# Turning the gated outputs with VectorE's 32x32 transposes instead of TensorE's, with a layout made by DMA

## The chip, the cores and the metric

The kernel runs on one core of a Trainium2 chip. The metric is the device time of one execution in microseconds (us), as the median of several runs; lower is better. The engines of a core work side by side, each in the order of its own queue: TensorE (PE for matmuls, PEld for its weight loads), VectorE (DVE), ScalarE (ACT), GpSimd (POOL) and SyncE (SP), which here issues nearly all DMAs.

## The reference

One layer of a streaming encoder over a prompt of 4096 frames and a sample of 64 frames, width 1024, in float32. What matters here is the end of the layer:

```
o_a = rms_norm(o_a, g_on_gla).reshape(B, T, 512) * silu(z_a)      # GLA branch, 4 heads of 128
o_h = rms_norm(o_h, g_on_hgrn).reshape(B, T, 512) * silu(z_h)     # HGRN2 branch, 4 heads of 128
o   = einsum('bte,ed->btd', concatenate([o_a, o_h]), w_out)       # w_out is 1024 x 1024
y   = x + gate * rms_norm(o, g_post)
```

`g_on_gla` and `g_on_hgrn` are gains of 128 values, the same for each head of their branch. Before that stand the adaLN modulation, one input projection and two chunked recurrences.

## The kernel before, in words

Matrix products run in fp32r on numbers split in two parts: `hi` is the rounded value (a cast on ACT), `lo` the rest (a subtraction, on DVE or POOL), and a product takes three matmuls (hi x w_hi, hi x w_lo, lo x w_hi). The function `split` (L84) makes both parts.

Frames are worked on in tiles of 128, two to a group of 256: 32 tiles of the prompt and one of 64 frames for the sample, which rides with the third group. There are three phases.

- Phase 1 (up to about 900 us) projects and runs the GLA recurrence. Its outputs, normalised without their gain and already multiplied by silu(z_a), are stored to DRAM as `oa_d` (L1109).
- Phase 2 (up to about 1600 us) does the same for HGRN2. Its outputs, normalised without gain and without silu(z_h), go to `oh_d`. While its last group is finished, the generator `load_wout` (L1198) loads w_out in 16 halves of [128 x 512] through the staging tiles `wst`, and splits each (the cast on ACT, L90; the rest on POOL, L91). In the same stretch the z projection of the first four tiles runs (`until(4)`).
- Phase 3 (`phase3`, L1218) goes tile by tile. `z_tile` (L1185) computes silu(z_h) of a tile some five tiles ahead: 24 matmuls (L571), a sigmoid on ACT (L1193) and a product on DVE (L1194) into a tile `e`. `load` brings the tile's GLA and HGRN outputs into `og` (L1215, L1216) and x into `xt`. `turn` (L1241) multiplies the HGRN half by `e` (L1244, called og*e below), turns the tile from frames on partitions to features on partitions with eight 128x128 TensorE transposes into two PSUM banks (`ps_tp`, `ps_ms`, L1252), and splits the result into `ogh` and `ogl`, with the gain of the output norm as a scalar per partition (L87, L88). Then come 48 matmuls with w_out (L1287) into two `pj` banks, a sum of squares on ACT (L1292), the products with the gate (L1296), rsqrt by Newton steps (L71 to L81), the sum with x (L1299) and the store of y (L1303).

The phases overlap by generators that are advanced in turn (`weave`). A scheduler in the framework orders the instructions of each engine: it takes the program's order as priority, and what is ready by its own estimate of durations. That order is fixed when the kernel is built; on the chip each queue goes strictly in it and waits where an operand is late. Tiles come from pools with a fixed number of buffers, and an instruction that writes a new tile waits until the tile that had this buffer is read for the last time. Numbers that matter: `og`, `ogh`, `ogl`, `y`, `xt` two buffers each, `e` five, PSUM `pj` three banks, `at` two (the z projection in phase 3). The buffers of phase 3 use the memory of the recurrences' tiles, so they are free only when phase 2 has ended.

Of the kernel before, what the change touches and what calls it, by code (L numbers as in the profile page):

```python
# [6 lines left out]
F32 = mybir.dt.float32  # L7
# [4 lines left out]
ALU = mybir.AluOpType  # L12
# [3 lines left out]
P = 128  # L16
# [12 lines left out]
class Kernel:  # L29
# [1167 lines left out]

    def load_wout(self, out):  # L1198

        sts = []  # L1200
        for i in range(2 * KT + 2):
            if i < 2 * KT:
                kt, n = divmod(i, 2)
                st = self.wst()[:, :512]
                self.nc.sync.dma_start(st, self.t["w_out"][0, kt * P : (kt + 1) * P, 512 * n : 512 * n + 512])
                sts.append(st)
            if i >= 2:
                out.append(self.split_w(sts[i - 2], "wv" if i - 2 < 8 else "wu", self.nc.gpsimd))
            yield

    def og_load(self, tile, og):

        g, j, (kind, _, r, _) = tile
        g = g if kind == "p" else -1
        self.nc.sync.dma_start(og[:r, :512], self.oa_d[g][j])  # L1215
        self.nc.sync.dma_start(og[:r, 512:], self.oh_d[g][j])  # L1216

    def phase3(self, tiles, zgen, og):  # L1218
        nc, t = self.nc, self.t
        with ExitStack() as s:  # L1220
            one = self.pool(s, "p3one")
            ap = self.pool(s, "p3a")
            gg = one.tile([P, 2, D], F32, name="gg")
            for i in range(2):
                nc.sync.dma_start(gg[:, i, :], self.gate_d[i : i + 1, :].to_broadcast([P, D]))
            Wo = self.W3["o"]
            og0 = og

            def load(i):
                g, j, (kind, r0, r, o) = tiles[i]  # L1230
                if i > 0:
                    og = ap.tile([P, D], F32, name="og", bufs=2)
                    self.og_load(tiles[i], og)
                else:
                    og = og0
                xt = self.xp.tile([P, D], F32, name="xt", bufs=2)
                src = t["x_prompt"] if kind == "p" else t["x_sample"]
                nc.sync.dma_start(xt[:r], src[0, r0 : r0 + r, :])
                return og, xt

            def turn(i, og):  # L1241
                r = tiles[i][2][2]
                e = self.zq.pop(0)
                nc.vector.tensor_tensor(og[:r, 512:], og[:r, 512:], e, ALU.mult)  # L1244
                hi = ap.tile([P, D], F32R, name="ogh", bufs=2).rearrange("p (k c) -> p k c", k=KT)
                lo = None
                if r == P:
                    lo = ap.tile([P, D], F32R, name="ogl", bufs=2).rearrange("p (k c) -> p k c", k=KT)
                for q, tag in enumerate(("tp", "ms")):
                    pt = self.ps(tag).rearrange("p (k c) -> p k c", k=4)  # L1250
                    for k in range(4):
                        nc.tensor.transpose(  # L1252
                            pt[:, k, :r], og[:r, (4 * q + k) * P : (4 * q + k + 1) * P], self.ident[:r, :r]
                        )
                    ks = slice(4 * q, 4 * q + 4)
                    self.split(hi[:, ks, :r], lo[:, ks, :r] if r == P else hi[:, ks, r : 2 * r], pt[:, :, :r], gain=self.col[:, 50 + q : 51 + q])
                return hi, lo

            n = len(tiles)
            og, xt = load(0)  # L1260
            next(zgen, None)
            hl = turn(0, og)
            for i in range(n):
                g, j, (kind, r0, r, o) = tiles[i]
                dst = t["y_prompt"] if kind == "p" else t["y_sample"]
                x_now, (hi, lo) = xt, hl
                if i + 1 < n:
                    next(zgen, None)
                    og, xt = load(i + 1)
                    hl = turn(i + 1, og)  # L1270
                cnd = 0 if kind == "p" else 1
                ss = self.small.tile([P, 2], F32, name="y_ss")[:r]
                y = ap.tile([P, D], F32, name="y", bufs=2)
                if i == n - 1:

                    self.tc.keep_in_program_order(nc.scalar.preload_act_table_set("natural_log_exp_and_others"))
                for q in range(2):
                    po = self.ps("pj")
                    cs = slice(512 * q, 512 * q + 512)
                    m = 0  # L1280
                    for kt in range(KT):
                        wh, wl = Wo[2 * kt + q][:, 0], Wo[2 * kt + q][:, 1]
                        if r < P:
                            self.pair_step(po, hi[:, kt, : 2 * r], r, wh, wl, kt)
                            continue
                        for a, b in ((hi, wh), (hi, wl), (lo, wh)):
                            nc.tensor.matmul(po[:r], a[:, kt, :r], b, start=m == 0, stop=m == 3 * KT - 1)  # L1287
                            m += 1
                    if r < P:
                        self.fold(po, r, 512, y[:, cs])  # L1290
                    junk = ap.tile([P, 512], mybir.dt.bfloat16, name="sq", bufs=1)[:r]
                    nc.scalar.activation(junk, po[:r], AF.Square, accum_out=ss[:, q : q + 1])  # L1292
                    if q:
                        nc.vector.tensor_tensor(ss[:, 0:1], ss[:, 0:1], ss[:, 1:2], ALU.add)
                        rs = self.rstd(ss[:, 0:1], D, table=i == n - 1)
                    nc.vector.tensor_tensor(y[:r, cs], po[:r], gg[:r, cnd, cs], ALU.mult)  # L1296
                for q in range(2):
                    cs = slice(512 * q, 512 * q + 512)
                    nc.vector.scalar_tensor_tensor(y[:r, cs], y[:r, cs], rs, x_now[:r, cs], ALU.mult, ALU.add)  # L1299
                    if i == n - 1:  # L1300
                        (nc.scalar if q else nc.sync).dma_start(dst[0, r0 : r0 + r, cs], y[:r, cs])
                if i < n - 1:
                    nc.sync.dma_start(dst[0, r0 : r0 + r, :], y[:r])  # L1303
# [189 lines left out]
```

## Time and profile before

| | |
|---|---|
| median of 3 runs | 2168.68 us (2168.2 to 2170.03) |
| the profiled execution | 2167.58 us, its span 2165.8 us |
| granted clock of TensorE | 0.995 of full speed on the mean |
| PE busy | 2121.3 us, 98% of the span |
| DVE / ACT / POOL busy | 1448.8 / 979.4 / 237.1 us |
| PE transposes in phase 3 (L1252), recorded | 256, of 264 issued |
| DMA engines, mean share busy | 24% by the main queue |

The page of the profile has parts: busy time by engine, the span in slices, the DMA queues, the chain of work that ended last (followed back from the last instruction to whatever released each step), the costliest groups of instructions, and DMA issues. A row of a group reads: line, engine, operation, output<-inputs, shapes, count, busy us and mean ns of one, then the idle time before them and what ended it. A row of a timeline reads: start in us from the span's start, duration, engine, line, operation, operands, count, and in brackets how long the engine had been idle and for what. A row of the chain reads: start, length, engine or DMA, tile, line, count.

### The profile page before, as it was taken

What the parts mean: (1) busy time and instruction counts of PE and PEld (TensorE: products, weight loads), DVE (VectorE), ACT (ScalarE), POOL (GpSimd) and SP (SyncE); (2) the same over time, 40 slices, a digit from 0 to 9 for tenths busy, and PEclk for the clock granted to TensorE, in tenths of its full rate; (3) what the DMA queues carried; (4) which work ended last, traced back from release to release, by engine and by line L of the source; (5) the groups of instructions that cost most, each with busy time, mean ns of one, the idle gap of its engine ahead of it and who ended that gap; (6) DMA issues with size and microseconds to landing.
All of it is one profiled execution on the core that took longest, in us unless ns stands there. A gap on an engine that the chain in (4) does not pass through costs nothing.

```text
span 2165.8 us, 44469 instructions
## 1 busy us (share of the span) xinstructions
PE 2121.3 (98%) x16776; PEld 1868.9 (86%) x16776; DVE 1448.8 (67%) x4735; ACT 979.4 (45%) x2790; POOL 237.1 (11%) x636
## 2 busy tenths in 40 slices
PE   7999999999999999999999999999989999999998
PEld 6898899999999888889899988999868888888887
DVE  6866666666666687777778877677894454545444
ACT  5665555655556564434444444444542222222212
POOL 3200010000110111110111111000230000000000
PEclk9999999999999999999999999999999999999999
DMA  9321111211111231011121111001343433333322
GB/s 269 118 76 55 55 50 60 79 55 55 50 60 65 89 102 42 30 40 58 58 70 46 35 31 50 31 31 42 99 151 119 127 128 107 127 112 131 109 102 87
DMA packets 98706, 173.15 MB, mean 80 GB/s; under 512 B 12668, under 2 KB 34656, under 8 KB 98492
## 3 DMA queue, kind: packets, MB, share of 16 engines
q1 hardware_dynamic: 98348, 170.05, 24.1%
q8 instruction: 132, 2.16, 0.4%
q14 instruction: 82, 0.67, 0.1%
q10 hardware_dynamic: 144, 0.26, 0.0%
HBM read 118.35 MB, written 51.93 MB: 79 GB/s over the span
## 4 chain that ended last, share of the span: by engine, by line
PE 86%; DVE 7%; ACT 3%; DMA 3%; issue 1%; POOL 0%; SPq 0%; DVEq 0%; ACTq 0%; POOLq 0%
PE ps_pj L571 22%; PE ps_pj L559 22%; PE ps_pj L1287 16%; PE ps_at L571 7%; PE ps_at L908 2%; PE ps_ms L791 2%; PE ps_at L638 2%; PE ps_o L775 2%; PE ps_o L770 2%; DMA xt<-in_x_prompt_dram 2%; DVE wst L861 1%; PE ps_tp L506 1%; PE ps_at L718 1%; PE ps_tp L745 1%; PE ps_pj L579 1%
## 5 line engine op out<-in xcount | busy, mean ns | idle before, releaser
L571 PE MATMUL ps_pj<-wu,hh 128*128 128x512 f32 x1632 | 405.3, 397 | 3.3 <-DVE hh L91 2.4
L559 PE MATMUL ps_pj<-hh,wu 128*128 128x256 f32 (+1 forms) x2976 | 395.6, 287 | 0.0
L559 PEld LDWEIGHTS ps_pj<-hh,wu 128*128 128x128 f32 x2976 | 373.8, 191 | 4.6 <-issue 0.3
L571 PEld LDWEIGHTS ps_pj<-wu,hh 128*128 128x128 f32 x1632 | 297.6, 188 | 65.5 <-issue 3.5
L559 PE MATMUL ps_pj<-hh,wv 128*128 128x256 f32 (+1 forms) x1536 | 214.1, 289 | 0.0
L559 PEld LDWEIGHTS ps_pj<-hh,wv 128*128 128x128 f32 x1536 | 192.5, 188 | 14.9 <-issue 12.9
L571 PE MATMUL ps_pj<-wv,hh 128*128 128x264 f32 x1464 | 203.2, 290 | 1.6 <-DVE wv L91 1.6
L571 PEld LDWEIGHTS ps_pj<-wv,hh 128*128 128x128 f32 x1464 | 184.5, 188 | 6.5 <-issue 3.1
L1292 ACT ACTIVATE sq<-ps_pj 128x512 bf16<-128x512 f32 (+1 forms) x66 | 39.4, 597 | 294.7 <-PE ps_pj L1287 289.7
L1287 PE MATMUL ps_pj<-wv,ogh 128*128 128x512 f32 x512 | 163.0, 399 | 0.0
L571 PE MATMUL ps_at<-wu,hh 128*128 128x512 f32 x672 | 158.5, 392 | 0.0
L1287 PE MATMUL ps_pj<-wu,ogh 128*128 128x512 f32 x512 | 157.9, 390 | 0.0
L90 ACT CAST hh<-hf 128x512 fp32r<-128x512 f32 (+1 forms) x188 | 117.7, 626 | 75.2 <-PE ps_pj L571 36.8
L571 PEld LDWEIGHTS ps_at<-wu,hh 128*128 128x128 f32 x672 | 126.9, 189 | 26.4
L91 DVE TENSOR_TENSOR hh<-hf,hh 128x512 fp32r<-128x512 f32 (+1 forms) x188 | 133.1, 710 | 14.2 <-ACT hh L90 12.8
L1153 ACT ACTIVATE g<-ps_pj 128x256 f32<-128x256 f32 (+1 forms) x128 | 49.4, 386 | 198.2 <-PE ps_pj L559 197.7
L861 DVE TENSOR_TENSOR wst<-wst,T 128x160 f32<-128x160 f32 (+4 forms) x480 | 118.1, 263 | 4.0
L1287 PEld LDWEIGHTS ps_pj<-wu,ogh 128*128 128x128 f32 x512 | 96.1, 188 | 20.7
L890 POOL COPY T<-T 128x16 f32<-128x16 f32 (+1 forms) x32 | 9.6, 299 | 942.3 <-DVE Qg L831 870.4
L1287 PEld LDWEIGHTS ps_pj<-wv,ogh 128*128 128x128 f32 x512 | 94.4, 189 | 19.1
L1287 PE MATMUL ps_pj<-wv,ogl 128*128 128x512 f32 x256 | 100.7, 394 | 0.0
L1287 PE MATMUL ps_pj<-wu,ogl 128*128 128x512 f32 x256 | 99.7, 390 | 0.0
(300 smaller groups left out, 3705.7 us busy)
## 6 DMA issues: line engine op xcount, KB each, us to landing
xt<-in_x_prompt_dram SPq DMA_DIRECT2D x64, 512.0 KB
hf<-h_d SPq DMA_DIRECT2D x128, 256.0 KB
h_d<-hf SPq DMA_DIRECT2D x64, 256.0 KB
out_y_prompt_dram<-y SPq DMA_DIRECT2D x31, 512.0 KB
wst<-in_w_in_dram SPq DMA_DIRECT2D x36, 256.0 KB
ada_st<-in_w_ada_dram SPq DMA_DIRECT2D x32, 256.0 KB
oa_d<-e SPq DMA_DIRECT2D x32, 256.0 KB
oh_d<-e SPq DMA_DIRECT2D x32, 256.0 KB
```

The costliest lines, as they stand in the source:

```text
L90: self.nc.scalar.copy(hi, src)
L91: (eng or self.nc.vector).tensor_tensor(lo, src, hi.bitcast(F32), ALU.subtract)
L559: self.nc.tensor.matmul(ps[:, :T], a, b, start=i == 0, stop=i == n - 1)
L571: self.nc.tensor.matmul(ps[:r, : c1 - c0], a, b, start=kt == 0 and i == 0, stop=kt == KT - 1 and i == 2)
L638: nc.tensor.transpose(pt[:, i * P : (i + 1) * P], D[:, c + i, :], self.ident)
L770: nc.tensor.matmul(po[h], A[:, c * 4 + h, :], v, start=h < n, stop=St is None and h == 4 - n)
L775: nc.tensor.matmul(o, Q[rows[s], c * G + g, :], St[rows[s], g, :], start=NS == 2 and not apart and h == 1, stop=h == 4 - NS or h == 3 and ...
L791: nc.tensor.matmul(pd[s * w : (s + 1) * w, g, :], kc[:CL, g, s * w : (s + 1) * w], vs[c][:CL, h * P : (h + 1) * P], start=not apart, stop= ...
L861: nc.vector.tensor_tensor(parts(dst), parts(src), t.unsqueeze(3).to_broadcast(shape), ALU.mult)
L908: nc.tensor.matmul(pas[s][rows, g0 + g], K[rr, 2 * pr + g, rows], Yt[rr, o : o + P], start=True, stop=True)
L1153: nc.scalar.activation(sg, pf[:, :T], AF.Sigmoid)
L1287: nc.tensor.matmul(po[:r], a[:, kt, :r], b, start=m == 0, stop=m == 3 * KT - 1)
```

## The change

The eight TensorE transposes of a tile are replaced. A 128x128 turn is done as a layout step between the quarters of 32 partitions, and a turn inside each 32x32 block. For the GLA half the layout step is made as the tile is loaded: four DMAs instead of one, each for 32 partitions, with pieces of 512 bytes, bring `og[32a+t, 128b+f] = oa[32b+t, 128a+f]`. The HGRN half must first be multiplied by `e` in the layout of frames, so its layout step comes after that product: 16 DMAs from SBUF to SBUF (32 partitions x 512 bytes each) into a new tile `oq` with one buffer. Then one VectorE transpose of 32x32 blocks for each half writes `oT` [128 x 512] (one buffer for both halves), and `split` reads that from SBUF instead of PSUM.

The features come out in another order: partition 32a+i of feature tile c holds feature 128a+32c+i of its half. w_out's rows are loaded in the same order, by four DMAs of 32 rows for each half-tile instead of one of 128. Since partitions of a feature tile no longer share the heads' gain index in the same way, the gain is no longer a scalar in `split`; it is loaded in the new order into a small tile (eight DMAs into 8 columns of an `e` tile) and multiplied into the w_out half on GpSimd, in place, before its split.

```diff
     def load_wout(self, out):
+        nc, t = self.nc, self.t
+        gain = self.etile()[:, :8]
+        for q, name in enumerate(("g_onorm_gla", "g_onorm_hgrn")):
+            src = t[name].rearrange("o (c i) -> i (o c)", c=4)
+            for a in range(4):
+                nc.sync.dma_start(gain[32 * a : 32 * a + 32, 4 * q : 4 * q + 4], src)
+        src = t["w_out"][0].rearrange("(q a c i) n -> q c a i n", q=2, a=4, c=4)
...
-                self.nc.sync.dma_start(st, self.t["w_out"][0, kt * P : (kt + 1) * P, 512 * n : 512 * n + 512])
+                for a in range(4):
+                    nc.sync.dma_start(st[32 * a : 32 * a + 32], src[kt // 4, kt % 4, a][:, 512 * n : 512 * n + 512])
                 sts.append(st)
             if i >= 2:
-                out.append(self.split_w(sts[i - 2], "wv" if i - 2 < 8 else "wu", self.nc.gpsimd))
+                st = sts[i - 2]
+                kt = (i - 2) // 2
+                nc.gpsimd.tensor_scalar(st, st, gain[:, kt : kt + 1], None, ALU.mult)
+                out.append(self.split_w(st, "wv" if i - 2 < 8 else "wu", nc.gpsimd))
...
     def og_load(self, tile, og):
-        self.nc.sync.dma_start(og[:r, :512], self.oa_d[g][j])
+        src = self.oa_d[g][j].rearrange("(b t) (a f) -> a t b f", t=32, a=4)
+        for a in range(4):
+            self.nc.sync.dma_start(
+                og[32 * a : 32 * a + 32, : r // 32 * P].rearrange("p (b f) -> p b f", f=P), src[a]
+            )
         self.nc.sync.dma_start(og[:r, 512:], self.oh_d[g][j])
...
             def turn(i, og):
                 r = tiles[i][2][2]
+                nb = r // 32
                 e = self.zq.pop(0)
                 nc.vector.tensor_tensor(og[:r, 512:], og[:r, 512:], e, ALU.mult)
+                oq = ap.tile([P, 512], F32, name="oq", bufs=1)
+                for a in range(4):
+                    for b in range(nb):
+                        nc.sync.dma_start(
+                            oq[32 * a : 32 * a + 32, b * P : b * P + P],
+                            og[32 * b : 32 * b + 32, 512 + a * P : 512 + a * P + P],
+                        )
...
-                for q, tag in enumerate(("tp", "ms")):
-                    pt = self.ps(tag).rearrange("p (k c) -> p k c", k=4)
-                    for k in range(4):
-                        nc.tensor.transpose(
-                            pt[:, k, :r], og[:r, (4 * q + k) * P : (4 * q + k + 1) * P], self.ident[:r, :r]
-                        )
+                for q, src in enumerate((og, oq)):
                     ks = slice(4 * q, 4 * q + 4)
-                    self.split(hi[:, ks, :r], ..., pt[:, :, :r], gain=self.col[:, 50 + q : 51 + q])
+                    oT = ap.tile([P, 512], F32, name="oT", bufs=1)[:, : 4 * r].rearrange("p (k c) -> p k c", k=4)
+                    nc.vector.transpose(
+                        oT.rearrange("p c (b t) -> p b c t", t=32),
+                        src[:, : nb * P].rearrange("p (b c i) -> p b c i", b=nb, i=32),
+                    )
+                    self.split(hi[:, ks, :r], ..., oT)
                 return hi, lo
```

More of the change, by code (lines that the diff above doesn't have):

```diff
@@ L1248, in turn @@
                     lo = ap.tile([P, D], F32R, name="ogl", bufs=2).rearrange("p (k c) -> p k c", k=KT)
-                for q, tag in enumerate(("tp", "ms")):
-                    pt = self.ps(tag).rearrange("p (k c) -> p k c", k=4)
-                    for k in range(4):
-                        nc.tensor.transpose(
-                            pt[:, k, :r], og[:r, (4 * q + k) * P : (4 * q + k + 1) * P], self.ident[:r, :r]
-                        )
-                    ks = slice(4 * q, 4 * q + 4)
-                    self.split(hi[:, ks, :r], lo[:, ks, :r] if r == P else hi[:, ks, r : 2 * r], pt[:, :, :r], gain=self.col[:, 50 + q : 51 + q])
+                for q, src in enumerate((og, oq)):
+                    ks = slice(4 * q, 4 * q + 4)
+                    oT = ap.tile([P, 512], F32, name="oT", bufs=1)[:, : 4 * r].rearrange("p (k c) -> p k c", k=4)
[3 more added lines that the diff above has]
+                    )
+                    self.split(hi[:, ks, :r], lo[:, ks, :r] if r == P else hi[:, ks, r : 2 * r], oT)
                 return hi, lo
```

## The prediction

> **What bounds the kernel now.** I read the page first (busy shares, then the chain that ended last), then a table of busy time by stretch to see where TensorE (PE) has room.
>
> ```profile
> PE 2121.3 (98%) x16776; PEld 1868.9 (86%) x16776; DVE 1448.8 (67%) x4735; ACT 979.4 (45%) x2790; POOL 237.1 (11%) x636
> PE 86%; DVE 7%; ACT 3%; DMA 3%; issue 1%; POOL 0%; SPq 0%; DVEq 0%; ACTq 0%; POOLq 0%
> ...
> 1540.00:1605.00 65.00, 58.77 (x423) 47.82 (x421) 61.35 (x148) 37.17 (x97) 25.69 (x31) 0.97 0.40 125
> 1605.00:1626.00 21.00, 17.31 (x76) 14.70 (x77) 15.90 (x45) 8.52 (x21) 5.78 (x11) 0.83 0.58 180
> ...
> 1700.00:1900.00 200.00, 200.00 (x929) 164.61 (x927) 101.04 (x278) 52.48 (x110) 0.00 (x0) 1.00 0.36 119
> ...
> 2088.00:2136.00 48.00, 48.00 (x231) 39.91 (x230) 21.80 (x64) 10.53 (x24) 0.00 (x0) 1.00 0.36 121
> ```
>
> The columns of the stretches are: length, busy time of PE, PEld, DVE, ACT, POOL, granted clock, DMA share, GB/s. The change lies in the last part (phase 3, from about 1615 us) and in the stage before it, where w_out is loaded. In phase 3 PE has no idle time at the full clock (200.00 of 200.00), DVE is half busy, POOL is empty. In 1540 to 1626 it is otherwise: DVE is 61.35 of 65 busy there and PE waits. So PE time taken away counts fully in phase 3, and nowhere else is there a promise. The chain shows what one tile costs:
>
> ```profile
> 1909.54 5.44 PE ps_at L571 x24
> 1914.98 0.44 PE ps_tp L1252 x4
> 1915.42 0.44 PE ps_ms L1252 x4
> 1915.86 10.98 PE ps_pj L1287 x48
> 1926.84 5.44 PE ps_at L571 x24
> ...
> 2112.58 10.98 PE ps_pj L1287 x48
> 2123.56 0.44 PE ps_tp L1252 x4
> 2124.00 0.44 PE ps_ms L1252 x4
> 2124.44 10.99 PE ps_pj L1287 x48
> ```
>
> A tile is 24 matmuls of the z projection, 8 transposes, 48 matmuls with w_out: 17.30 us from z to z. The last tiles have no z: 11.86 us. The transposes take 0.88 us of each.
>
> **The change, part by part.**
>
> *The eight TensorE transposes go.* 33 tiles; those of tiles 0 and 1 lie in the entry to phase 3, which I cost apart. 31 x 0.88 = 27.3 us off the path, if PE finds its operands in time. The period would be 16.42 us, and 10.98 in the tail. What must stay inside that:
>
> ```profile
> 1862.87 0.34 SPq L1303 DMA_DIRECT2D out_y_prompt_dram<-y  x1
> ...
> 1863.99 0.53 SPq L1215 DMA_DIRECT2D og<-oa_d  x1
> 1864.56 1.21 SPq L1216 DMA_DIRECT2D og<-oh_d  x1
> ...
> 1870.12 0.69 DVE L1244 TENSOR_TENSOR og<-og,e 128x512 f32<-128x512 f32 x1 [4.36 <-DMA og<-oh_d]
> 1870.73 0.68 DVE L1296 TENSOR_TENSOR y<-ps_pj,gg 128x512 f32<-128x512 f32 x1
> ...
> 67.44 1.25 SPq L404 DMA_DIRECT2D e<-in_w_alpha_dram  x3
> ...
> 2101.12 0.42 SPq L1216 DMA_DIRECT2D og<-oh_d  x1
> 2104.39 0.69 DVE L1244 TENSOR_TENSOR og<-og,e 128x512 f32<-128x512 f32 x1
> ...
> L91 DVE TENSOR_TENSOR hh<-hf,hh 128x512 fp32r<-128x512 f32 x24 | 16.4, 685 | 0.3 <-issue 0.3
> L88 DVE SCALAR_TENSOR_TENSOR ogl<-ps_ms,col,ogh 128x512 fp32r<-128x512 f32 x11 | 8.1, 740 | 0.0
> L90 ACT CAST hh<-hf 128x512 fp32r<-128x512 f32 x24 | 15.0, 624 | 11.4 <-PE ps_at L571 11.4
> ...
> q1 hardware_dynamic: 98348, 170.05, 24.1%
> ```
>
> *SP's queue.* Small DMAs follow each other every 1.25 / 3 = 0.42 us. A tile now issues 6 (y store, x load, two og loads, two of h on the mean); it will issue 25 (og in 5, and 16 for `oq`): 10.5 us of 16.42. In the tail 23, 9.7 us of 10.98: full, but it fits. Without its cover it would cost what it lies over.
>
> *DVE.* 101.04 / 200 x 17.30 = 8.74 us a tile. Two transposes of 128x512 are in no row; the nearest is the 685 ns of a two-input operation SBUF to SBUF of that shape (L91). Below I allow half of it, above twice; I take 0.69 each, since shape and memory are the same: +1.4 us. The low parts go from 740 ns to L91's 685: -0.1. So 10.0 us of 16.42, hidden under PE, and 11.4 with both at twice that. ACT's casts read SBUF in place of PSUM, at the 624 ns that L90 takes from there: nothing to pay. The Trainium skill ("VectorE: DVE Perf Modes", section "The three transpose paths") gives 311 ns for a 128x128 bf16 transpose on VectorE; four of these make an estimated 1.24 us, and DVE would need 11.1 us: the sum is the same. No run so far shows it.
>
> *The DMA engines.* 24.1% of 16 engines over 2165.8 us for 98348 packets is 85 ns a packet. 384 more packets for og (512 B instead of 2 KB) and 512 for oq are at most 896 x 85 / 16 = 4.8 us a tile, above the 36% now: about two thirds. No bound.
>
> *The new wait.* The transpose of the HGRN half waits for 16 DMAs: 16 x 0.42 = 6.7 us of issue, plus landing, which the rows at 2101.12 and 2104.39 put at no more than 2.85 us: 9.5 us. Behind it in DVE's queue stand its low part, the y products and the z product; for the first y product PE waits only when it needs that PSUM bank again (three `pj` banks, two a tile: about one tile later). In SP's queue the 16 wait for the product og*e, and behind them stand y stores and x and h loads. How much room there is: `ogh`/`ogl` have two buffers, so tile k's halves can be split once block k-2 has ended, and are needed after block k-1, 16.42 us later. `oq` is free again when tile k's second transpose is done, about 3 to 6 us into that time, and its 9.5 us for tile k+1 end before the next block does. So the waits cost nothing if the queues are in that order. `oT` with one buffer makes transpose, cast and low part of the two halves follow each other: 2 x (0.69 + 0.62 + 0.69), 4 us, in the same room. In the tail the room is 10.98 us: 4 + 9.5 overlaps the next tile's, but oq is still a block ahead. Taken as 0.
>
> *w_out.* 16 loads become 64 on SP (+20 us of issue), plus 8 small gain loads; POOL gets 16 products in place before ACT's cast.
>
> ```profile
> L91 POOL TENSOR_TENSOR wv<-wst,wv 128x512 fp32r<-128x512 f32 x8 | 12.4, 1573 | 25.6 <-ACT wv L90 25.6
> L284 POOL MEMSET zero<- 128x512 f32 x1 | 0.5, 531 | 0.0
> ...
> 1560.30 0.86 SPq L1205 DMA_DIRECT2D wst<-in_w_out_dram  x2
> 1566.28 0.33 SPq L527 DMA_DIRECT2D hf<-h_d  x1
> ...
> 1566.28 2.55 DMA hf<-h_d
> ...
> 1615.37 0.32 SPq L1225 DMA_DIRECT2D gg<-gate_d  x1
> 1622.34 0.43 SPq L1216 DMA_DIRECT2D og<-oh_d  x1
> ...
> 1620.41 4.77 DMA og<-oa_d
> 1625.32 1.09 PE ps_tp L1252 x4
> ...
> 1638.07 3.68 PE ps_at L579 x16
> ```
>
> A product on POOL lies between 0.53 (a fill) and 1.57 us (two inputs): 8 to 25 us, beside 25.69 busy of 65. Room enough. But one load on SP is on the chain, hf at 1566.28. Seven w_out halves are issued before it: 7 x 3 x 0.42 = 8.8 us more could push it; SP stands still from 1561.16 to 1566.28 in front of it, so I take 0 and keep 0 to +8.8.
>
> *The entry.* Now the first block of 48 begins in earnest after tile 1's transposes waited for og (1620.41, 4.77 us), and ends at 1638.07. Afterwards block 0 does not wait for tile 1, but its second half of feature tiles waits for oq of tile 0. That can be issued when phase 3's memory is free (the gg load, 1615.37). If the 16 come right behind the two gg loads, from 1616.2: + 6.7 + 2.85 + 0.69 + 0.62 = 1627.1, and the 36 matmuls left (36/48 of 10.98, 8.2 us) end at 1635.3: -3. If they come behind the og loads of two more tiles (1622.77, and 2.5 us for six more issues), from 1625.3: 9 us later, +6. Between the two I take 0.
>
> Sum: 27.3 us gained, 0 for entry and w_out. The profiled execution took 2167.58 us (span 2165.8), the median of the runs shown is 1.1 us above: 2168.7 - 27.3 = 2141.4, so 2141.
>
> **The rivals.**
>
> *The queues form a loop (slower).* The scheduler may put og*e of a later tile ahead of the next tile's transposes on DVE. Then each turn goes: HGRN transpose, 16 issues and landing of the next oq (9.5), release of og, five og loads and landing (4.9 by the tail rows; 7.4 by 1863.99 to 1870.12 with three more issues), then on DVE the product, a y product, a low part, the transpose (2.8). Sum 17.2 to 19.7, middle 18.5. It decides from 16.42 on. Against 17.30 it costs 27 tiles x 1.2 and, against 11.86, 4 x 6.6: +59, 2228 (2188 to 2262). For it: DVE already waits 4.36 us for og in front of work. Against it: how the order is made.
>
> ```profile
> 1848.78 0.51 SPq L1216 DMA_DIRECT2D og<-oh_d  x1
> 1852.93 0.69 DVE L1296 TENSOR_TENSOR y<-ps_pj,gg 128x512 f32<-128x512 f32 x1 [3.29 <-ACT sq L1292]
> 1854.34 0.69 DVE L1244 TENSOR_TENSOR og<-og,e 128x512 f32<-128x512 f32 x1 [0.71 <-DMA og<-oh_d]
> ```
>
> Here the y product was put first and og*e found its load nearly landed; a tile later og*e came first (1870.12, then 1870.73). The order follows the landing to within a microsecond or two, so what the scheduler assumes of DMAs is near the chip's, and it will see these 16 as well.
>
> *The gain is eaten at the entry and by w_out.* Both upper ends, 6 + 8.8: 2156.
>
> *No change.* PE could fall to a lower clock or be held by weight loads. The clock is 1.00 and PEld 165 of 200; the transposes also have weight loads. 2168.
>
> *Each small DMA waits for the one before.* 16 x (0.42 + 2.85) = 52 us a tile: 27 x 35 + 4 x 40, about 3270 us. Against it: three issues in 1.25 us. The Trainium skill ("DMA: Bandwidth & Descriptors", section "Rules for kernel authors") says to coalesce many small transfers, since under 64 KB mostly overhead is paid; these are 16 KB. By its fixed cost of 2.0 us each, one after another, it would be an estimated 33 us a tile. The trace agrees on the size of the overhead, not on its being paid in turn.
>
> **How the numbers follow.** Forecast 0.64, entry and w_out 0.10, no change 0.05, loop 0.19, one by one 0.02. Faster 0.74, same 0.05, slower 0.21; 0.2% (4 us) is about what a measurement of this kernel can tell. Range: below, the sum with some 7 us from entry and waits around 1605 to 1626: 2134. Above, through the entry case and no change, to just short of the loop: 2185. That leaves out about 0.2. The likeliest's own range is 2134 to 2150.
>
> **What would show it.** Right: no L1252; chain of 5.44 and 10.98 in turn, 16.42 from z to z; PE 200 of 200 in a window of phase 3; 25 SP issues a tile; DVE near 61% with transposes of about 0.7 us. Wrong: PE waiting for `ogh` or `ogl`; DVE's largest wait on oq's DMA, above 6 us a tile; SP's `oq` issues waiting for og*e with a y store behind; block 0 ending after 1640; hf loads late behind w_out. If the 16 issues take 0.6 us each rather than 0.42, SP is over its 10.98 us in the tail.

## The result, and the profile after

The changed kernel takes 2223.98 us (median of 4 runs, 2221.89 to 2225.39), the kernel before beside it on the same chip 2169.36 (2168.20 to 2170.25): a ratio of 1.0249, 95% interval 1.0236 to 1.0263. It is 55 us slower, where I had forecast 27 us faster. The profiled span is 2223.6 us.

From the page, the busy times and the shares by engine of the chain that ended last; then the stretches, with the columns as before:

```profile
PE 2118.9 (95%) x16512; PEld 1846.5 (83%) x16512; DVE 1489.7 (67%) x4801; ACT 977.9 (44%) x2790; POOL 263.7 (12%) x652
...
PE 60%; SPq 16%; DVE 8%; DMA 8%; issue 3%; ACT 3%; POOL 1%; DVEq 0%; POOLq 0%; ACTq 0%
```

```profile
1540.00:1605.00 65.00, 54.82 (x405) 43.31 (x404) 52.67 (x146) 30.58 (x76) 30.00 (x33) 0.97 0.36 105
...
1605.00:1660.00 55.00, 48.02 (x231) 39.91 (x232) 30.54 (x76) 20.56 (x54) 27.98 (x25) 0.88 0.36 109
1700.00:1900.00 200.00, 189.26 (x803) 148.78 (x802) 109.48 (x280) 49.02 (x105) 0.00 (x0) 0.99 0.47 135
2088.00:2136.00 48.00, 41.31 (x168) 32.62 (x167) 23.48 (x58) 8.94 (x20) 0.00 (x0) 0.93 0.38 115
```

PE has 264 instructions less, the transposes (33 tiles of 8), and yet it now stands still in phase 3: 189.26 of 200.00 where it was 200.00 of 200.00, 41.31 of 48 in the tail. SP's queue, 0% of the chain before, holds 16% of it. Who waits, from the table of waits (engine and line, what it waited for, us in all, times, longest):

```profile
ACT ogh L90 <- DVE oT L1278: 333.9, 56, 12.9
...
DVE oT L1278 <- DMA oq<-og: 128.4, 31, 7.4
...
PE ps_pj L1313 <- ACT ogh L90: 55.7, 32, 5.1
```

PE waits for the split halves (`ogh`), ACT for the transpose, the transpose for `oq`'s DMAs, 31 times. Behind that stands SP. Its timeline over one tile of the tail, the piece of the chain at the same place, and the row of the `oq` issues of all tiles but the first (duration min / median / max in ns, first and last start):

```profile
2131.52 10.01 SPq L1267 DMA_DIRECT2D oq<-og  x16
2141.62 0.53 SPq L1329 DMA_DIRECT2D out_y_prompt_dram<-y  x1
2142.20 1.26 SPq L1230 DMA_DIRECT2D og<-oa_d  x2
2143.50 0.48 SPq L1233 DMA_DIRECT2D og<-oh_d  x1
2144.02 0.43 SPq L1255 DMA_DIRECT2D xt<-in_x_prompt_dram  x1
2144.56 0.84 SPq L1230 DMA_DIRECT2D og<-oa_d  x2
2147.09 10.75 SPq L1267 DMA_DIRECT2D oq<-og  x16
```

```profile
2143.50 2.84 DMA og<-oh_d
2146.37 0.70 DVE og L1263
```

```profile
L1267 SPq DMA_DIRECT2D oq<-og x504: 507/589/1770, 1651.9 to 2204.7; - x168
```

This is a closed loop, and it lies in SP's program order: 16 issues of one tile (10.0 us, one every 0.63), then y's store, then the `og` loads of the next tile, which were written behind them; `og`'s HGRN half lands 2.84 us after its issue, og*e takes 0.70, and only then may the next 16 be issued. 2131.52 to 2147.09 is 15.6 us a turn. The product's own rows on VectorE give the period over many tiles:

```profile
1755.14 0.67 DVE L1263 TENSOR_TENSOR og<-og,e 128x512 f32<-128x512 f32 x1
...
2082.86 0.65 DVE L1263 TENSOR_TENSOR og<-og,e 128x512 f32<-128x512 f32 x1
...
2098.37 0.69 DVE L1263 TENSOR_TENSOR og<-og,e 128x512 f32<-128x512 f32 x1 [0.24 <-DMA og<-oh_d]
...
2193.92 0.69 DVE L1263 TENSOR_TENSOR og<-og,e 128x512 f32<-128x512 f32 x1 [0.20 <-DMA og<-oh_d]
```

The first two are 18 tiles apart: 18.2 us a tile with z, against 17.30 before. That is a mean: turns of about 16 and 20 us alternate, and in a long one (products at 1704.67 and 1724.26) two h loads go out between the 16 issues and the `og` loads, and `og`'s half lands 4.92 us after its issue. The last two are 6 tiles apart: 15.9 us, against 11.86. About 25 tiles x 0.9 and 6 x 4.0 are 47 us; the entry to phase 3 is 7.7 us later: here the first block of 48, with two z projections (16 and 24 matmuls) run inside it, gave way to the second at 1654.87; before, the block and the 16 were done at 1641.75, and 5.44 for the other z make 1647.2. PE's timeline, and on SP the load that marks the start of phase 3 (1615.37 before):

```profile
1643.91 5.61 PE L571 MATMUL ps_at<-wu,hh 128*128 128x512 f32 x24
...
1654.87 0.39 PE L1313 MATMUL ps_pj<-wv,ogh 128*128 128x512 f32 x1
```

```profile
1632.65 0.84 SPq L1242 DMA_DIRECT2D gg<-gate_d  x2
```

47 and 7.7 are, within rounding, the 55 us.

### The profile page after: what moved, and what is told of

Read it like the earlier page. It is cut to its first block, busy times and chain, and to the rows that moved or that the text cites. A ratio compares the mean times of both kernels' runs of the same rounds, so it can differ in the third digit from the quotient of the medians.

```text
span 2223.6 us, 44804 instructions
## 1 busy us (share of the span) xinstructions
PE 2118.9 (95%) x16512; PEld 1846.5 (83%) x16512; DVE 1489.7 (67%) x4801; ACT 977.9 (44%) x2790; POOL 263.7 (12%) x652
## 4 chain that ended last, share of the span: by engine, by line
PE 60%; SPq 16%; DVE 8%; DMA 8%; issue 3%; ACT 3%; POOL 1%; DVEq 0%; POOLq 0%; ACTq 0%
PE ps_pj L571 22%; PE ps_pj L559 21%; SPq L1267 13%; DMA og<-oh_d 3%; PE ps_ms L791 2%; PE ps_at L908 2%; PE ps_at L638 2%; PE ps_o L775 2%; PE ps_o L770 2%; PE ps_pj L1313 2%; DMA xt<-in_x_prompt_dram 1%; DVE wst L861 1%; SPq L1230 1%; PE ps_at L718 1%; PE ps_tp L506 1%
## 5 line engine op out<-in xcount | busy, mean ns | idle before, releaser
L1313 PE MATMUL ps_pj<-wu,ogh 128*128 128x512 f32 x512 | 169.8, 419 | 47.9 <-ACT ogh L90 47.7
L559 PEld LDWEIGHTS ps_pj<-hh,wv 128*128 128x128 f32 x1536 | 192.5, 188 | 14.9 <-issue 12.9
L90 ACT CAST ogh<-oT 128x512 fp32r<-128x512 f32 (+1 forms) x66 | 40.4, 611 | 333.9 <-DVE oT L1278 333.9
L1278 DVE STREAM_TRANSPOSE oT<-oq 128x512 f32<-128x512 f32 (+1 forms) x33 | 23.2, 703 | 131.2 <-DMA oq<-og 128.4
```

Of the source, the lines that this page charges most:

```text
L90: self.nc.scalar.copy(hi, src)
L559: self.nc.tensor.matmul(ps[:, :T], a, b, start=i == 0, stop=i == n - 1)
```

## The experiments

Two theories of phase 3 at first: the loop through SP's 16 issues (Q), or DMAs that wait for one another whoever issues them (L). For the entry: GpSimd's product (W), or something else. "Before" is 2168.56, 2168.67, 2168.81 and 2170.11 us in the four groups of runs.

**e1: half the issues.** Eight transfers of 64 partitions in place of 16 of 32, the same bytes. They put the features and frames in another order, so this kernel does not compute the layer's prompt output; it is there for its time alone.

```diff
-    for a in range(4):
-        for b in range(nb):        # 32 partitions -> 32 partitions
+    for a in range(2):
+        for b in range(4):         # 64 -> 64
```

> The layout of the HGRN half is made by 8 DMAs of 64 partitions x 512 bytes a tile instead of 16 of 32 partitions: the same bytes, but the frames and features land in another order, so the outputs of the prompt are not the reference's. Theory Q (SyncE's queue sets phase 3: 16 issues at 0.63 us, then the next og loads, their landing and og*e, one after the other): 8 issues less are 5.0 us less a tile, the period of tiles with z falls from 18.2 to TensorE's own 16.4 us and that of the last tiles from 15.9 to about 11.0; total 2151 us. Rival D (the order on VectorE binds, its transposes and products in turn): period stays near 18, total above 2200 us.

Measured: 2146.44 us, ratio 0.9896 (0.9876 to 0.9915). Its stretch, its chain, and its row of issues:

```profile
1700.00:1900.00 200.00, 200.00 (x879) 163.78 (x878) 114.98 (x311) 53.36 (x115) 0.00 (x0) 1.00 0.54 152
```

```profile
1866.95 5.44 PE ps_at L571 x24
1872.39 10.97 PE ps_pj L1319 x48
```

```profile
L1268 SPq DMA_DIRECT2D oq<-og x248: 461/595/1432, 1643.6 to 2109.1; - x124
```

PE is full again, and the chain is the one that I had forecast: 5.44 and 10.97 in turn, 16.41 from z to z. The price per issue is the same 0.59 us for twice the partitions and bytes, so between these two it is paid per issue, not per byte.

**e2: two issuers.** The 16 stay, half of them on ACT's queue.

```diff
-    nc.sync.dma_start(
+    (nc.scalar if (a + b) % 2 else nc.sync).dma_start(
```

> The 16 DMAs of a tile are issued half by SyncE and half by ScalarE. Theory Q (issue time on one queue): 5.0 us less on SyncE a tile, period 16.4, total about 2151 us if ScalarE's casts do not get stuck behind its 8 issues. Rival L (each DMA waits until the one eight before it has landed, whichever queue issues it): no gain, 2224 us. Rival S (ScalarE's queue stands behind the wait for og*e, and casts and sigmoids come late): 2224 us or slower, with waits for ScalarE on TensorE.

Measured: 2155.02 us, 0.9928 (0.9908 to 0.9949); PE 200.00 of 200.00 between 1700 and 1900. ACT's issues take as long as SP's:

```profile
L1267 SPq DMA_DIRECT2D oq<-og x252: 507/588/1330, 1649.0 to 2122.6; - x126
L1267 ACTq DMA_DIRECT2D oq<-og x252: 514/601/1842, 1653.6 to 2123.1; - x126
```

The same DMAs of the same size, and 69 us less: L falls. What costs is that one queue issues them in a row. The Trainium skill ("DMA: Bandwidth & Descriptors", section "Issuing engines are not separate DMA queues") says that several issuers only save the time to initiate a DMA, "usually small relative to the DMA itself". That this time is saved agrees with the run; that it is small does not carry over: 0.59 us an issue, 16 times in a row, are 10.0 of the 15.6 us of a turn.

**e3: the og loads ahead.** The loads of tile i+2 are written in front of the 16 issues of tile i+1, so that they land, and their product can be made, while these are issued. The number of issues on SP stays.

```diff
+    og = load_og(1)
     for i in range(n):
         if i + 1 < n:
-            og, xt = load(i + 1)
-            hl = turn(i + 1, og)
+            xt, og_now = load(i + 1), og
+            if i + 2 < n: og = load_og(i + 2)
+            hl = turn(i + 1, og_now)
```

> Only the order of the program changes: the og loads of a tile are issued before the 16 DMAs of the tile before it, so that they land while these are issued. Theory Q with the landing in the turn: landing (2.9 us) and og*e (0.7 us) leave SyncE's turn, 18.2 falls to 16.4 us (TensorE) and the last tiles' 15.9 to 12.3; total about 2158 us. Rival Q2 (the 16 issues alone are the bound, with what else SyncE issues): period 17 to 18, total above 2195 us.

Measured: 2188.33 us, 1.0089 (1.0070 to 1.0109), between the two forecasts. The stretch, two rows of 16 issues in the tail, and what such rows waited for:

```profile
1700.00:1900.00 200.00, 195.60 (x851) 157.99 (x850) 117.87 (x302) 51.76 (x110) 0.00 (x0) 1.00 0.50 138
```

```profile
2104.65 10.25 SPq L1267 DMA_DIRECT2D oq<-og  x16
...
2119.88 11.41 SPq L1267 DMA_DIRECT2D oq<-og  x16
```

```profile
SPq L1267 <- DMA xt<-in_x_prompt_dram: 25.0, 25, 2.1
```

The order of the loads is worth 36 us, two thirds of the loss: the loop was real. What is left lies mostly in the tail, where a turn still takes 15.2 us (2104.65 to 2119.88), against 15.6 in the changed kernel and 10.98 of PE's work: SP's own issues alone, 13.6 us by the rows of the changed kernel's turn (10.01, 0.53, 1.26, 0.48, 0.43 and 0.84), are more than PE needs. The 16 themselves take between 10.0 and 13.1 us here; in 25 tiles one of them waits for the landing of x's load just ahead, 1 us on the mean. Why an `oq` issue should wait for x's load no run here tells.

**e4: GpSimd's product moved to ACT.**

```diff
-    nc.gpsimd.tensor_scalar(st, st, gain[:, kt : kt + 1], None, ALU.mult)
+    nc.scalar.activation(st, st, AF.Copy, scale=gain[:, kt : kt + 1])
```

> The products of w_out with the gains move from GpSimd to ScalarE. Theory W (the stage before phase 3 is bound by GpSimd, 16 x (1.7 + 1.35) us): the entry comes some 8 us earlier, total about 2216 us, phase 3's period unchanged at 18.2. Rival: the entry waits for SyncE's 64 loads and 8 gain loads: 2224 us.

Measured: 2225.67 us, 1.0251 (1.0228 to 1.0274): no change, W as I had put it fell. GpSimd's busy time between 1540 and 1605 went from 30.00 to 17.90 us, and the first tile's `oq` issues began at 1632.39 in place of 1635.25, but of these 2.9 us nothing reached the end.

**e5: the w_out part alone**, put on the kernel before: 64 loads, 8 gain loads, the product; TensorE's transposes stay.

```diff
+    for a in range(4):
+        nc.sync.dma_start(st[32*a : 32*a+32], rows(kt, a))     # rows in their old places
...
+    nc.gpsimd.tensor_scalar(st, st, gain[...], None, ALU.mult)
-    self.split(hi, lo, pt, gain=self.col[:, 50 + q : 51 + q])
+    self.split(hi, lo, pt)
```

> The kernel before with the w_out part of the change alone: each half row block by four loads of 32 rows (rows in their old places), eight gain loads, the product on GpSimd, and no gain in the split of phase 3. Theory W (the 56 further issues on SP hold back everything issued behind them, gg, hf, og): the first block of 48 ends at about 1646 in place of 1638.07, and the time is 2168.6 + 7.7 = 2176 us (2173 to 2181). Rival O (what is late at the entry is late because of the first tile's 16 oq transfers): 2169 us, within 3.

Measured: 2175.44 us, 1.0031 (1.0020 to 1.0042): 6.8 us, all of it at the entry (PE 200.00 of 200.00 afterwards).

**e6: the GLA half alone.** No `oq`; the HGRN half goes through four TensorE transposes.

```diff
-    oq = ...; 16 x dma_start(oq <- og)
+    for k in range(4):
+        nc.tensor.transpose(pt[:, k, :r], og[:r, (4 + k) * P : (5 + k) * P], self.ident[:r, :r])
```

> Only the GLA half of the gated output goes the new way (four loads by quarters, one 32x32 transpose on VectorE); the HGRN half is turned by four TensorE transposes as before, so the 16 oq transfers are gone. Theory Q (the loop through SP's 16 issues is the whole loss of phase 3): 0.44 us a tile less on PE, 16.86 us with z and 11.42 without, PE 200 of 200 between 1700 and 1900; 31 x 0.44 = 13.6 us gained, less about 4 us at the entry (24 further w_out issues of 48): 2159 us (2154 to 2164). Rival (the four og loads by quarters or the VectorE transposes hold PE up as well): 2169 us or more, with DVE waiting on og's loads.

Measured: 2153.73 us, 0.9928 (0.9912 to 0.9945), PE 200.00 of 200.00. The 15 us are the 13.6 forecast without the loss at the entry that I had set against them, although the GLA half of w_out still has its small loads, its late gains and eight of the 16 products. The loads by quarters and the VectorE transposes hold nobody up.

**e7: by way of DRAM.** One store of the HGRN product, four loads by quarters: 5 issues for 16.

```diff
-    for a in range(4):
-        for b in range(nb):
-            nc.sync.dma_start(oq[32a.., b*P..], og[32b.., 512 + a*P ..])
+    nc.sync.dma_start(d, og[:r, 512:])
+    d = d.rearrange("(b t) (a f) -> a t b f", t=32, a=4)
+    for a in range(4):
+        nc.sync.dma_start(oq[32a..] as "p b f", d[a])
```

> The HGRN product goes back to DRAM by one store and comes in by quarters with four loads: 5 issues in place of 16, and two landings one behind the other in place of one. Theory Q by my sum of SP's turn: store 0.4, landing 2.9, four loads 1.9, y and x and og issues 3.2, landing 2.85, product 0.7: about 12 us, under 16.42 with z and over 10.98 in the tail. PE full between 1700 and 1900, 2169 - 27.3 + 7.7 + 6 x 1.3 = 2157 us (2149 to 2165). Rival D (landings weigh more than issues, so two in a row undo it): DVE waits for oq more than in the changed kernel, 2200 us or more.

Measured: 2150.75 us, 0.9912 (0.9895 to 0.9930). Its stretch, its loads and its stores:

```profile
1700.00:1900.00 200.00, 200.00 (x879) 163.77 (x878) 114.15 (x310) 53.13 (x113) 0.00 (x0) 1.00 0.58 172
```

```profile
L1270 SPq DMA_DIRECT2D oq<-oh_d x132: 302/426/1138, 1631.3 to 2107.3; - x132
```

```profile
L1267 SPq DMA_DIRECT2D oh_d<-og x32: 319/338/483, 1645.2 to 2097.1; - x32
```

Two landings one behind the other are hidden, 16 issues were not. A load from DRAM costs 0.43 us of issue and a store 0.34, a copy from SBUF to SBUF 0.59. In the tail too PE is full (48.00 of 48 between 2088 and 2136), better than the 12 us a turn that I had summed.

**e8: fewer, larger w_out loads, gains early**, on the version with two issuers.

```diff
-    for a in range(4): nc.sync.dma_start(st[32a..], half row block)       # 64
+    for a in range(4): nc.sync.dma_start(pair[32a..], full row block)     # 32
-    gain = self.etile()[:, :8]       # loaded in front of w_out
+    gain = self.gain                 # loaded with the constants
```

> The oq issues alternate between SP and ACT as in e2_act, and w_out comes in by 32 loads of 32 full rows in place of 64 of half rows, with the gains loaded at the start of the kernel. Theory W (SP's w_out issues set the entry): block 0 ends some 4 to 12 us earlier than in e2_act, 2147 us (2141 to 2152). Rival O (the first tile's oq transfers set it): 2155 us, as e2_act, within 3.

Measured: 2153.40 us, 0.9926 (0.9911 to 0.9940), 1.6 us from the 2155.02 without: in this version neither the number of w_out issues nor the late gains set the entry. PE's longest wait there is this one:

```profile
1635.39 4.21 PE L586 MATMUL ps_at<-wu,hs 128*128 128x512 f32 x9 [14.30 <-POOL hs L555]
```

`hs` is a cast of the sample's frames on GpSimd, and stands in GpSimd's queue behind products and low parts of w_out, one of which itself waited 7.68 us for its load. e2 has the same wait, 11.19 us. So GpSimd's work on w_out still held PE here.

**e10 and e11: issues or product?** The two halves of the w_out part, each alone on the kernel before.

```diff
 e10:  + four loads of 32 rows for each half row block, no gain loads, no product
 e11:  + gain loads and product on GpSimd, loads as before
```

> The kernel before with 64 w_out loads of 32 rows in place of 16 of 128 rows, and nothing else: no gain loads, no product. Theory I (SP's issues make the 6.8 us of e5_wout): 2175 us (2173 to 2178). Theory P (the product in each staging slot's turn makes them): 2168.6 us, within 3.

> The kernel before with 16 w_out loads as before, the eight gain loads, the product on GpSimd in front of the cast, and no gain in the split of phase 3. Theory I: 2168.6 us, within 3, a little less if anything. Theory P: 2175 us (2173 to 2178), since each staging slot's turn holds 1.6 us more of GpSimd.

Measured: 2159.89 us, 0.9966 (0.9952 to 0.9980) with the issues alone; 2182.29, 1.0066 (1.0049 to 1.0082) with the product alone. Theory I is refuted with the wrong sign, and P was too low by half. The stretches of before (the first stands in the prediction), of e10 and of e11:

```profile
1605.00:1660.00 55.00, 51.31 (x230) 42.38 (x231) 32.05 (x89) 15.99 (x37) 5.78 (x11) 0.91 0.43 139
```

```profile
1540.00:1605.00 65.00, 60.63 (x431) 49.22 (x431) 58.10 (x152) 36.93 (x94) 20.19 (x29) 0.95 0.39 109
1605.00:1660.00 55.00, 53.00 (x247) 42.62 (x246) 31.12 (x85) 18.36 (x41) 8.96 (x14) 1.00 0.56 183
```

```profile
1540.00:1605.00 65.00, 57.09 (x416) 45.49 (x414) 49.61 (x147) 30.24 (x78) 31.59 (x34) 0.92 0.36 110
1605.00:1660.00 55.00, 41.20 (x214) 33.79 (x214) 34.21 (x79) 22.52 (x58) 27.76 (x25) 0.91 0.46 143
```

PE's busy time by its granted clock is an estimate of the work done: 58.77 x 0.97 + 51.31 x 0.91 = 103.7 us before, 110.6 in e10, 90.0 in e11. So e10 has done 6.9 us more of it by 1660, and e11 13.7 less, which is where their 8.9 and 13.5 us are; the two together, 4.6 us, are near the 6.8 of e5, which has both. And e11's GpSimd, from the groups by line between 1540 and 1640, with two rows of its table of waits there and PE's longest wait:

```profile
L1218 POOL TENSOR_SCALAR wst<-wst,e 128x512 f32<-128x512 f32 x16 | 29.0, 1821 | 28.0 <-DMA e<-in_g_onorm_hgrn_dram 21.9 <-DMA wst<-in_w_out_dram 6.1
...
ACT wv L90 <- POOL wst L1218: 18.1, 8, 4.8
ACT wu L90 <- POOL wst L1218: 9.3, 5, 2.9
...
1639.48 1.09 PE L1263 MATMUL ps_tp<-ident,og 128*128 128x128 f32 x4 [11.13 <-DVE hh L91]
```

The first product begins at 1560.27, when the last gain loads have landed; these stand on SP behind the first w_out loads and behind a store of phase 2 (1557.00). Of the 21.9 us of waiting the greater part is time in which GpSimd had nothing to do before either (its first low part began at 1550.95 in the kernel before), so the lateness is some 9 us. After that each of the 16 products takes 1.8 us in a row of load, product, cast and low part through four staging slots, and ACT waits 27.4 us for them. Phase 2's last work stands in the same queues: its last store of `oh_d` goes out at 1636.01 in place of 1620.05, and PE waits 11.13 us in front of the transposes. Why smaller loads are better than large ones, e10's 8.9 us, no run tells.

**e12, all together:** by way of DRAM, 32 w_out loads, gains loaded with the constants, and the gain put into the cast (ACT) and the low part (VectorE) of w_out, so that there is no product.

```diff
-    nc.gpsimd.tensor_scalar(st, st, gain[:, kt : kt + 1], None, ALU.mult)
-    out.append(self.split_w(st, tag, nc.gpsimd))
+    self.split(w[:, 0], w[:, 1], st, gain=gain[:, kt : kt + 1])
```

> e7_bounce with the w_out part made light: 32 loads of full rows, gains loaded at the start, and the gain applied in the cast (ACT) and in the low part (VectorE, 0.74 us) so that GpSimd has neither product nor low part. If theory P holds, the entry is back at the time of before: 2150.75 - 7 = 2144 us (2140 to 2149). If theory I holds, half of the issues are gone: 2147 us. Rival: VectorE, 0.82 busy in that stage, pays 16 x 0.74 = 12 us for it: 2151 us or more.

Measured: 2133.20 us (2131.16 to 2134.46), 0.9838 (0.9824 to 0.9853): 35.6 us faster than before, the fastest version here, and beyond what either theory gave it.

```profile
1540.00:1605.00 65.00, 63.80 (x498) 52.75 (x497) 59.54 (x184) 40.74 (x105) 5.93 (x18) 1.00 0.40 118
1605.00:1660.00 55.00, 50.69 (x211) 39.46 (x210) 34.68 (x87) 17.84 (x37) 2.41 (x8) 0.97 0.60 186
1700.00:1900.00 200.00, 200.00 (x879) 163.83 (x878) 117.55 (x322) 54.12 (x114) 0.00 (x0) 1.00 0.55 170
```

By the prediction's sum 27.3 us are the transposes. The rest is the entry: 113.0 us of work by 1660 in the measure above, 9.3 more than before, GpSimd nearly empty (5.93 us) and VectorE, which took on the low parts, at 59.54 of 65 no busier than the 61.35 before. Of the issues of theory I half are gone, of the product of theory P all, and of the late gains too; GpSimd's low parts are gone with them, and the gains no longer hold one of the five `e` buffers through this stage. No run takes these apart.

**e13, the loop by itself:** the changed kernel with that light w_out part.

```diff
 e12 with the 16 copies og -> oq on SP put back
```

> The changed kernel with the light w_out part of e12_best and nothing else: the 16 oq transfers of a tile stay on SP. Theory S (two losses that add: the loop through SP's 16 issues, and the w_out part): the step from e7_bounce to e12_best, 17.5 us, comes off the changed kernel too: 2224 - 17.5 = 2206 us (2200 to 2212), with the period still at 18.2 us with z. Rival M (the entry is covered by the first tiles' oq transfers, so that the w_out part costs little here): 2216 to 2224 us.

Measured: 2208.34 us, 1.0180 (1.0163 to 1.0197).

```profile
1700.00:1900.00 200.00, 188.65 (x802) 148.83 (x801) 109.00 (x281) 47.63 (x103) 0.00 (x0) 0.99 0.43 131
```

The losses add, nearly: the light w_out part takes 15.6 us off the changed kernel, which has the loop, and 17.5 off e7, which has not. From e12 to e13 the loop costs 75.1 us. Written out against before, -35.6 + 75.1 + 15.6 = +55.1.

## Why the prediction was wrong, step by step

- **"So the waits cost nothing", "Taken as 0"** is the step that failed. It listed what stands behind the 16 issues on SP, "y stores and x and h loads", and left out the `og` loads of the next tile, on which the next product and so the next 16 wait. With them the turn closes: 10.0 of issue, about 2 for y and `og` issues, 2.84 landing, 0.70 product, 15.6 us in the tail. "if the queues are in that order" named the condition, and a reading of the loop that issues (load, then turn, one tile after the other) would have shown that it does not hold. The loop costs 75.1 us (e13 against e12).
- **"16 x 0.42 = 6.7 us of issue"** took the price of small loads from DRAM for copies from SBUF to SBUF. Those took 0.59, one every 0.63 us, 10.0 in all: the sentence "if the 16 issues take 0.6 us each" in my own list of signs. The loads from DRAM kept to it (0.43 in e7). The order and the price decided together. At 6.7 us for the 16 the same turn would be, as an estimate from the turns above, 12.3 us in the tail and 14.9 with z: under PE's 16.41 with z, and 1.3 us over its 10.98 in the tail. With the measured price and another order (e3) the loss is 20 us in place of 55, most of it in the tail, where "full, but it fits" is wrong by this price alone: 13.6 us of issues for 10.98.
- **The rival "the queues form a loop"** is what happened, and its 2228 us is near 2224, but partly by luck: it put the loop into VectorE's order, with 9.5 + 4.9 + 2.8, and charged nothing to w_out. It lies in SP's order, is cheaper for it (18.2 with z, where it had 18.5, and 15.9 in the tail), and w_out pays the rest. The argument against it, that the scheduler orders VectorE by the landings, fits VectorE (in 20 of the turns it still stands idle for `og`'s load in front of the product, 7.5 us in all) and says nothing of SP, whose order is that of the loop.
- **w_out, "I take 0 and keep 0 to +8.8"**: 6.8 alone (e5), inside that range. The 15.6 of the changed kernel are against e13's light part, which is itself some 8 us better at the entry than the kernel before. I looked for the price in SP's 48 further issues; those by themselves gain 8.9 (e10). The price is in the product and the late gains (13.5, e11). "Room enough" counted GpSimd's busy share and missed that each half waits its turn there, and ACT's casts with it (27.4 us in e11). Of the two, e4 (product off GpSimd) and e8 (gains early) mended nothing by itself, e6 with half of the products lost nothing, and e12, with neither product nor late gains, gained; which share belongs to which stays open.
- **The entry, "Between the two I take 0"**: block 0 was not done at 1640, the sign that I had named. It is w_out's lateness, not the `oq` of the first tile: e5 has it without any `oq`.
- **The eight transposes, 31 x 0.88 = 27.3 us:** right, or nearly: e7 lies 24.7 us under e5, which has the same w_out part and TensorE's transposes. Wherever SP's row of 16 is broken up, PE is full and the period is 16.41 (e1, e7, e12), as summed.
- **VectorE's transposes at 0.69 each:** 0.703 on the mean, by the groups of the changed kernel:

```profile
L1278 DVE STREAM_TRANSPOSE oT<-oq 128x512 f32<-128x512 f32 (+1 forms) x33 | 23.2, 703 | 131.2 <-DMA oq<-og 128.4
```

 The nearest row was the right one, the estimate of 1.24 us from the Trainium skill ("VectorE: DVE Perf Modes", "The three transpose paths") too high.
- **"One by one", 3270 us:** refuted; the 16 transfers of a tile start 0.63 us apart, and the transpose that needs them all begins 1.9 us after the last is started (2125.20 to 2127.07), so several are in flight at a time. Of the rule of the Trainium skill to coalesce ("DMA: Bandwidth & Descriptors", "Rules for kernel authors") the advice was right here: one store of 256 KB and four loads of 64 KB in place of 16 copies of 16 KB took 73 us off (e7 against the changed kernel). But e2 took 69 off with the 16 small copies as they were, so it was the issues in a row on one queue that cost, not the size of the transfers.

## What to carry to other kernels

Count the issues of a queue per tile, price them by a row of the same kind of transfer (source and destination), and then write down the queue's order around one whole turn: a transfer that waits for a product, whose input is loaded behind that transfer's predecessors on the same queue, is a loop, and its period is the sum of all of it. A rearrangement of many small copies was better done here as one store and a few wide loads, or spread over two issuers. And an operation put on an idle engine is not free where its operands pass through few buffers: a share of busy time does not show that.

## What the runs showed of the hardware that was not expected

An issue on SP's queue took 0.34 us for a store to DRAM (e7; y's store right behind the row of copies took 0.53), 0.42 for a load of 32 partitions, and 0.59 for a copy from SBUF to SBUF, of 32 partitions as of 64; a w_out load of 32 full rows also took 0.59 (e12). What makes the difference no run tells.

A wait can cost PE more than its length. In the tail of the changed kernel, by PE's timeline (the idle time before an instruction in brackets):

```profile
2144.35 1.22 PE L1313 MATMUL ps_pj<-wu,ogh 128*128 128x512 f32 x2 [4.61 <-ACT ogh L90]
2145.36 0.63 PE L1313 MATMUL ps_pj<-wu,ogl 128*128 128x512 f32 x1
...
2146.64 0.63 PE L1313 MATMUL ps_pj<-wu,ogl 128*128 128x512 f32 x1
...
2149.00 0.39 PE L1313 MATMUL ps_pj<-wu,ogl 128*128 128x512 f32 x1
...
2149.70 0.40 PE L1313 MATMUL ps_pj<-wu,ogl 128*128 128x512 f32 x1
```

After 4.61 us of waiting, a matmul with the low part takes 0.63 us in place of 0.40, until about 2149; three matmuls then take 1.28 (2145.36 to 2146.64) and not the 0.70 from 2149.00 to 2149.70. The granted clock from 2144.35 to 2149.00 is 0.53 of full speed, and a like wait of 4.63 us at 2112.66 lies in the stretch above whose clock is 0.93. The length of the wait alone does not decide: after 3.14 us (2160.79) such a matmul takes 0.39, after 2.22 us (1821.12) 0.63. The Trainium skill ("TensorE: Matmul & The Clock Gate", section "Part 1: The HAM clock gate") says that the array runs at half its clock after an idle window of about 3.4 us, until some 3.4 us of work have passed, and that the window runs freely. The trace agrees on about half the rate, for 4.65 us; the wait of 2.22 us that brought it on is shorter than that window.
